# Storing the token difference feature-major and building the shifted inputs with one multiply-add

## The chip, the cores and the metric

The kernel runs on one core of a Trainium2 chip. The metric is device time in microseconds (us) of one execution. Three runs of the kernel before took 2236.38, 2239.85 and 2240.13 us; their median is 2239.85 us.

## The reference, cut to what matters

One inference step of two layers over 1024 prompt tokens and 8 sample tokens, 1024 features wide. Layer 0 ends in an output projection and a layer norm; its result `x` is the input of layer 1, a recurrent (RWKV-7) layer. That layer mixes every token with the token before it, six times with six weight vectors `mu`, and projects each mix:

```
x_prev = concatenate([shift_prev[:, None], x[:, :-1]], axis=1)      # the token before; a stored row for the samples
xsh = x[None] + (x_prev - x)[None] * mu[:, None, None, :]           # six shifted inputs
r, k, v, z = einsum('nbtd,nde->nbte', xsh[:4], w_rkvz)
w_raw = -softplus(-(w0 + tanh(xsh[4] @ w1) @ w2)) - 0.5             # "sigma" in the kernel
a = sigmoid(a0 + (xsh[5] @ a1) @ a2)
# then the recurrence over tokens, a group norm, a gate by z, the output projection and a layer norm
```

For the prompt the token before token 0 is zero; each of the 8 samples is one token whose predecessor is a row of `state_shift`.

## The kernel before, in words

The kernel has four phases, A to D. A and B compute layer 0 up to its branches, phase C its output projection and layer norm, phase D all of layer 1. The program is written in order and then reordered by a scheduler, engine by engine: each engine then works through its own fixed list, and waits at an instruction until its operands are there and the buffer that it writes is free. TensorE is PE, VectorE DVE, ScalarE ACT, GpSimd POOL; SP is the queue that issues most DMAs.

**Phase C** (`phase_c`) handles nine tiles, eight of 128 tokens and one of the 8 samples, in the order t = 0 to 8. For each it loads `x` and the branch outputs, splits them into a high and a low float32r part, does 48 matmuls of 512 columns (L1073 to L1075), the layer norm (`ln_core`, L1027 to L1036), the gain and bias on POOL (L1078, L1079), eight transposes on PE (L1090) that ACT copies out (L1091) as the feature-major tile `xt`, and one store of `xt` to the DRAM scratch `x1T` (L1094). `x1T` exists twice: half 0 for tokens 0 to 511, half 1 for the rest and the samples. The buffers of a tile (`x`, `h`, `xt` and others) come in pairs.

**Phase D** (`phase_d`) begins with five projections for half 0, in the order in which `FSEQ` interleaves them: k, sigma, r, a, v. After them the recurrence runs over 16 units, with the projections of half 1 and later the z projections and the output filled in between. Each projection starts with `xmake(h, i)` (from L1187): for each of the 8 blocks `k` of 128 features it loads 512 or 520 tokens of `x1T` into `xk` at column 1 (L1196), puts the predecessor of the first token into column 0 on POOL (L1198 zero, L1200 from `G.last`), scales on ACT by `1 - mu` into `xs` (L1201), adds `mu` times the neighbour column on DVE (L1202, and L1204 for the 8 samples), and splits the sum into `xh` (ACT, L1205) and `xl` (L1206, POOL, or DVE for every second block in the first five projections). `xmake` runs 12 times, 96 blocks in all. A projection k, r, v or z then takes 8 output blocks `j`, each with 8 x 3 matmuls per chunk of 256 tokens (L1178 to L1180), and stores each block (L1309).

A tile pool of phase D takes the bytes that earlier pools have left. A tile that lies on bytes of a phase C tile can be written only when that tile's last reader is done.

Of the kernel before, what the change touches and what calls it, by code (L numbers as in the profile page):

```python
# [8 lines left out]
F32 = mybir.dt.float32  # L9
# [1030 lines left out]
def phase_c(nc, tc, I, O, G):  # L1040
    ident = G.C["ident"]
    scr = G.scr
    with ExitStack() as es:
        pool = lambda name, bufs, **k: es.enter_context(tc.tile_pool(name=name, bufs=bufs, reuse_waits="tile", **k))
        one = pool("c1", 1)
        sp = pool("c2", 2)
        ps, woh, wol = G.ps, G.woh, G.wol
        gB = one.tile([128, D], F32, name="gB")
        bB = one.tile([128, D], F32, name="bB")
        nc.sync.dma_start(gB, I["ln_rows"][0:1].to_broadcast([128, D]))  # L1050
        nc.sync.dma_start(bB, I["ln_rows"][2:3].to_broadcast([128, D]))
        gT = one.tile([128, 2, 8], F32, name="gT")
        nc.sync.dma_start(gT, I["ln_cols"])
        for t in range(9):
            r = 128 if t < 8 else NS
            x = sp.tile([128, D], F32, name="x")
            nc.sync.dma_start(x[0:r], I["xp"][t * 128:t * 128 + 128] if t < 8 else I["xs"])
            yh = sp.tile([128, 8, 128], F32R, name="yh")
            yl = sp.tile([128, 8, 128], F32R, name="yl")
            y8 = sp.tile([128, 8, 128], F32, name="y8")  # L1060
            nc.sync.dma_start(y8[:, 0:4, 0:r], scr["ya"][:, :, t * 128:t * 128 + r])
            nc.sync.dma_start(y8[:, 4:8, 0:r], scr["yb"][:, :, t * 128:t * 128 + r])
            zt = sp.tile([128, 4, 128], F32, name="zt")
            nc.sync.dma_start(zt[:, :, 0:r], scr["za"][:, :, t * 128:t * 128 + r])
            nc.gpsimd.tensor_tensor(y8[:, 0:4, 0:r], y8[:, 0:4, 0:r], zt[:, :, 0:r], op=MUL)
            for i in (0, 4):
                sv = y8[:, i:i + 4, 0:r]
                split(nc, yh[:, i:i + 4, 0:r], yl[:, i:i + 4, 0:r], sv, nc.scalar, nc.vector if i else nc.gpsimd)
            a = ps.tile([128, 1024], F32, name="S")
            for n in range(2):  # L1070
                sl = slice(n * 512, n * 512 + 512)
                for k in range(8):
                    nc.tensor.matmul(a[0:r, sl], lhsT=yh[:, k, 0:r], rhs=woh[:, k, sl], start=k == 0, stop=False)  # L1073
                    nc.tensor.matmul(a[0:r, sl], lhsT=yh[:, k, 0:r], rhs=wol[:, k, sl], start=False, stop=False)
                    nc.tensor.matmul(a[0:r, sl], lhsT=yl[:, k, 0:r], rhs=woh[:, k, sl], start=False, stop=k == 7)  # L1075
            h = ln_core(nc, sp, a, x, r)
            x1 = x
            nc.gpsimd.tensor_tensor(x1[0:r], h[0:r], gB[0:r], op=MUL)  # L1078
            nc.gpsimd.tensor_tensor(x1[0:r], x1[0:r], bB[0:r], op=ADD)  # L1079
            nc.scalar.dma_start(scr["x1"][t][0:r], x1[0:r])  # L1080
            if t == 7:
                nc.scalar.dma_start(O["shift_p"], x1[127:128])
            if t == 8:
                nc.scalar.dma_start(O["shift_s"], x1[0:r])
            xt = sp.tile([128, 8, 128], F32, name="xt")
            for half in range(2):
                pt = ps.tile([128, 512], F32, name="mm")
                for kk in range(4):
                    k = half * 4 + kk
                    nc.tensor.transpose(pt[:, kk * 128:kk * 128 + r], h[0:r, k * 128:k * 128 + 128], ident[0:r, 0:r])  # L1090
                    nc.scalar.activation(xt[:, k, 0:r], pt[:, kk * 128:kk * 128 + r], AF.Identity,  # L1091
                                         scale=gT[:, 0, k:k + 1], bias=gT[:, 1, k:k + 1])
            q, c0 = (t // 4, (t % 4) * 128) if t < 8 else (1, 512)
            nc.sync.dma_start(scr["x1T"][q][:, :, c0:c0 + r], xt[:, :, 0:r])  # L1094
            if t == 3:
                nc.vector.tensor_copy(G.last, xt[:, :, 127:128])


def phase_d(nc, tc, I, O, G):
# [5 lines left out]
    with ExitStack() as es:  # L1105
# [20 lines left out]
        K = {k: cc[:, o:o + n] for k, (o, n) in G.offc.items()}  # L1126
        mu = one.tile([128, 6, 8], F32, name="mu")
        nc.sync.dma_start(mu, I["mu"])
        omu = one.tile([128, 6, 8], F32, name="omu")
        nc.vector.tensor_scalar(omu, mu, -1.0, 1.0, op0=MUL, op1=ADD)  # L1130
        shT = one.tile([128, 8, NS], F32, name="shT")
        nc.sync.dma_start(shT, I["shT"])
        vec = one.tile([128, 8, 7], F32, name="vec")
        nc.sync.dma_start(vec[:, :, 0:5], I["vec"])
        nc.vector.tensor_scalar(vec[:, :, 5:6], vec[:, :, 1:2], 0.5, None, op0=MUL)
# [51 lines left out]
        def xmake(h, i):  # L1187
# [3 lines left out]
            for k in range(8):  # L1191
                hi.append(xp.tile([128, 520], F32R, name="xh"))
                lo.append(xp.tile([128, 520], F32R, name="xl"))
                t = sp.tile([128, 520], F32, name="xs")
                x = one.tile([128, 528], F32, name="xk", bufs=3)
                nc.sync.dma_start(x[:, 1:1 + n], scr["x1T"][h][:, k, 0:n])  # L1196
                if h == 0:
                    nc.gpsimd.memset(x[:, 0:1], 0.0)  # L1198
                else:
                    nc.gpsimd.tensor_copy(x[:, 0:1], G.last[:, k])  # L1200
                nc.scalar.activation(t[:, 0:n], x[:, 1:1 + n], AF.Copy, scale=omu[:, i, k:k + 1])  # L1201
                nc.vector.scalar_tensor_tensor(t[:, 0:512], x[:, 0:512], mu[:, i, k:k + 1], t[:, 0:512], op0=MUL, op1=ADD)  # L1202
                if h:
                    nc.vector.scalar_tensor_tensor(t[:, 512:n], shT[:, k], mu[:, i, k:k + 1], t[:, 512:n], op0=MUL, op1=ADD)  # L1204
                nc.scalar.activation(hi[k][:, 0:n], t[:, 0:n], AF.Copy)  # L1205
                (nc.vector if early[0] and k % LD == 0 else nc.gpsimd).tensor_tensor(lo[k][:, 0:n], t[:, 0:n], hi[k][:, 0:n], op=SUB)  # L1206
            return hi, lo
# [332 lines left out]
        def sample_d():  # L1540
# [36 lines left out]
            sa = late.tile([128, 64], F32, name="sa")  # L1577
            y = late.tile([128, 64], F32, name="ys")
            for v0 in range(0, 64, 8):
                S = one.tile([128, 8, 64], F32, name="xk", bufs=3)  # L1580
                t = one.tile([128, 8, 64], F32, name="xk", bufs=3)
                vs = slice(v0, v0 + 8)
                kb = lambda i: R[:, i].unsqueeze(1).to_broadcast([128, 8, 64])
                vb = lambda a: a[:, vs].unsqueeze(2).to_broadcast([128, 8, 64])
# [117 lines left out]
        def t_out(g):  # L1702
# [19 lines left out]
                nc.sync.dma_start(h[ti], scr["x1"][2 * g + ti])  # L1722
            H = [[x[:, 0:512], x[:, 512:]] for x in h]
            if g == 2:
                H.append([one.tile([128, 512], F32, name="xk", bufs=3) for _ in range(2)])
                for f in range(2):
                    nc.sync.dma_start(H[2][f][0:NS], scr["x1"][8][0:NS, f * 512:f * 512 + 512])
            st = sp.tile([128, 3, 8], F32, name="st")
# [78 lines left out]
def body(tc, I, O, stage="all"):  # L1807
# [4 lines left out]
    with ExitStack() as es:  # L1812
# [7 lines left out]
        for nm, v in (("eps_ln", LN_EPS), ("eps_gn", GN_EPS), ("eps_kk", 1e-30)):  # L1820
            C[nm] = cp.tile([128, 1], F32, name=nm)
            nc.gpsimd.memset(C[nm], v)
        G.last = cp.tile([128, 8, 1], F32, name="last")
        G.scr = {"x1": [dp.tile([128, D], F32, name=f"x1_{t}") for t in range(9)],
                 "x1T": [dp.tile([128, 8, 512 + NS * q], F32, name=f"x1T_{q}") for q in range(2)],
                 **{k: dp.tile([128, 4, TT], F32, name=k) for k in ("ya", "za", "zb", "q", "yb")},
                 "sgs": dp.tile([NS, D], F32, name="sgs")}
        with ExitStack() as eC:
# [17 lines left out]
            phase_c(nc, tc, I, O, G)  # L1846
        if stage == "C":
            for q in range(2):
                nc.sync.dma_start(O["d_x1T"][:, :, q * 512:q * 512 + 512], G.scr["x1T"][q][:, :, 0:512])
            return  # L1850
        phase_d(nc, tc, I, O, G)

# [81 lines left out]
```

## Time and profile before

| what | us |
|---|---|
| median of three runs | 2239.85 |
| profiled execution: span from first to last instruction | 2226.9 |
| PE busy | 1841.2 (83%) |
| DVE busy | 1605.9 (72%) |
| ACT busy | 1145.9 (51%) |
| POOL busy | 1024.0 (46%) |
| DMA engines busy (main hardware queue) | 32.2% |

The page describes one execution; of its own time it gives the span, and the median of the runs is 12.95 us above that. Busy times are sums over stages with different limits, so the prediction reads stages, as windows of the span. Phase C begins on PE at about 880 us, the first matmul of phase D starts at 990.85 us, the recurrence at 1240 us, and the last `xmake` block is made at 1818 us.

### The profile page before, as it was taken

What the parts mean: (1) busy time and instruction counts of PE and PEld (TensorE: products, weight loads), DVE (VectorE), ACT (ScalarE), POOL (GpSimd) and SP (SyncE); (2) the same over time, 40 slices, a digit from 0 to 9 for tenths busy, and PEclk for the clock granted to TensorE, in tenths of its full rate; (3) what the DMA queues carried; (4) which work ended last, traced back from release to release, by engine and by line L of the source; (5) the groups of instructions that cost most, each with busy time, mean ns of one, the idle gap of its engine ahead of it and who ended that gap; (6) DMA issues with size and microseconds to landing.
All of it is one profiled execution on the core that took longest, in us unless ns stands there. A gap on an engine that the chain in (4) does not pass through costs nothing. (4 is left out here: it accounts for less than half of the span.)

```text
span 2226.9 us, 41589 instructions
## 1 busy us (share of the span) xinstructions
PE 1841.2 (83%) x15802; PEld 1536.7 (69%) x15802; DVE 1605.9 (72%) x3103; ACT 1145.9 (51%) x2279; POOL 1024.0 (46%) x877
## 2 busy tenths in 40 slices
PE   5988897668998996997779998789989967987944
PEld 4987896656767775766669886579878646765532
DVE  5998994558788886246364678976579899888453
ACT  3323324554665554467475557765564664554433
POOL 4667666545655544535345213344234354123333
PEclk8998998868999975998779997789899777997867
DMA  6424444521221115545566343454334434342532
GB/s 233 135 74 139 136 143 152 199 72 45 64 59 52 56 47 151 156 143 162 177 195 192 112 113 106 128 163 140 108 104 132 125 115 154 86 144 76 172 110 97
DMA packets 234657, 276.32 MB, mean 124 GB/s; under 512 B 72057, under 2 KB 174129, under 8 KB 230298
## 3 DMA queue, kind: packets, MB, share of 16 engines
q1 hardware_dynamic: 213272, 216.26, 32.2%
q0 software_dynamic: 7616, 41.52, 5.6%
q10 hardware_dynamic: 13570, 15.90, 2.0%
q8 instruction: 124, 2.03, 0.4%
q14 instruction: 75, 0.61, 0.1%
HBM read 213.52 MB, written 64.27 MB: 125 GB/s over the span
## 5 line engine op out<-in xcount | busy, mean ns | idle before, releaser
L121 POOL TENSOR_TENSOR wl<-w,wh 128x1024 fp32r<-128x1024 f32 x81 | 199.0, 2457 | 267.3 <-ACT wh L113 229.6
L1178 PE MATMUL mm<-xh,wh 128*128 128x256 f32 (+1 forms) x1024 | 306.7, 301 | 13.7 <-ACT og L1307 5.0
L1179 PE MATMUL mm<-xl,wh 128*128 128x256 f32 (+1 forms) x1024 | 305.0, 298 | 4.8 <-POOL xl L1206 4.1
L1180 PE MATMUL mm<-xh,wl 128*128 128x256 f32 (+1 forms) x1024 | 301.0, 294 | 0.0
L113 ACT ACTIVATE wh<-w 128x1024 fp32r<-128x1024 f32 (+2 forms) x130 | 134.5, 1034 | 188.8 <-DMA w<-in_w_fm 63.5
L1178 PEld LDWEIGHTS mm<-xh,wh 128*128 128x128 f32 x1024 | 200.7, 197 | 24.8 <-ACT og L1307 6.5
L1179 PEld LDWEIGHTS mm<-xl,wh 128*128 128x128 f32 x1024 | 202.1, 197 | 12.3 <-POOL xl L1206 4.9
L1180 PEld LDWEIGHTS mm<-xh,wl 128*128 128x128 f32 x1024 | 202.0, 197 | 4.8 <-issue 2.9
L268 DVE SCALAR_TENSOR_TENSOR c<-U,cw,c 128x1024 f32<-128x1024 f32 x120 | 198.1, 1674 | 0.9
L604 POOL TENSOR_TENSOR Pl<-PT,Ph 128x512 fp32r<-128x512 f32 (+1 forms) x102 | 131.5, 1293 | 142.0 <-DVE Ph L603 116.0
L252 POOL TENSOR_TENSOR cbuf<-cbuf 128x256 f32<-128x256 f32 (+2 forms) x72 | 131.6, 1835 | 86.9 <-ACT cbuf L250 83.9
L217 PE MATMUL S<-xh,wh 128*128 128x344 f32 (+1 forms) x432 | 147.0, 340 | 23.8 <-ACT wh L113 12.5
L219 PE MATMUL S<-xh,wl 128*128 128x344 f32 (+1 forms) x432 | 145.3, 336 | 17.2 <-POOL wl L121 11.5
L218 PE MATMUL S<-xl,wh 128*128 128x344 f32 (+1 forms) x432 | 146.1, 338 | 3.6 <-POOL xl L121 3.4
L250 ACT ACTIVATE cbuf<-cbuf,wrow 128x256 f32<-128x256 f32 x192 | 79.3, 496 | 111.4 <-DMA cbuf<-in_ccmp,cix 79.8
L1206 POOL TENSOR_TENSOR xl<-xs,xh 128x520 fp32r<-128x520 f32 (+1 forms) x76 | 104.0, 1371 | 54.6 <-ACT xh L1205 52.9
L1202 DVE SCALAR_TENSOR_TENSOR xs<-xk,mu,xs 128x512 f32<-128x512 f32 x96 | 95.7, 1000 | 45.0 <-ACT xs L1201 42.5
L1417 DVE TENSOR_TENSOR ut<-uc,MT 128x16 f32<-128x16 f32 (+14 forms) x240 | 109.9, 458 | 20.1 <-POOL MT L1411 11.0
L217 PEld LDWEIGHTS S<-xh,wh 128*128 128x128 f32 (+1 forms) x432 | 85.4, 198 | 25.8 <-ACT wh L113 24.6
L562 DVE TENSOR_REDUCE nm<-S 128x1 f32<-128x640 f32 (+7 forms) x128 | 88.3, 699 | 17.1 <-PE S L558 16.0
L219 PEld LDWEIGHTS S<-xh,wl 128*128 128x128 f32 (+1 forms) x432 | 84.9, 196 | 21.8 <-POOL wl L121 13.7
L121 DVE TENSOR_TENSOR wl<-w,wh 128x1024 fp32r<-128x1024 f32 x45 | 57.8, 1285 | 44.4 <-ACT wh L113 44.4
(605 smaller groups left out, 5539.1 us busy)
## 6 DMA issues: line engine op xcount, KB each, us to landing
w<-in_w_rkvz SPq DMA_DIRECT2D x64, 512.0 KB
w<-in_w_out SPq DMA_DIRECT2D x36, 512.0 KB
w<-in_w_fm SPq DMA_DIRECT2D x25, 512.0 KB
xk<-x1T SPq DMA_DIRECT2D x48, 260.0 KB
xk<-x1T SPq DMA_DIRECT2D x48, 256.0 KB
w<-in_w_out SPq DMA_DIRECT2D x16, 256.0 KB
x<-in_xp SPq DMA_DIRECT2D x8, 512.0 KB
x<-x ACTq DMA_DIRECT2D x8, 512.0 KB
```

The source lines that it names most:

```text
L113: nc.scalar.activation(hi, src, AF.Copy, **({} if scale is None else {"scale": scale}))
L121: e_lo.tensor_tensor(lo, src, hi, op=SUB)
L217: nc.tensor.matmul(dst, lhsT=wh[:, k, 0:n], rhs=xh[:, k, sl], start=k == 0, stop=False)
L218: nc.tensor.matmul(dst, lhsT=wh[:, k, 0:n], rhs=xl[:, k, sl], start=False, stop=False)
L219: nc.tensor.matmul(dst, lhsT=wl[:, k, 0:n], rhs=xh[:, k, sl], start=False, stop=k == 7)
L252: nc.gpsimd.tensor_tensor(bv[:, 0:n], bv[:, 0:n], bv[:, n:2 * n], op=ADD)
L268: e.scalar_tensor_tensor(c[:, i, 0:T], u[:, k:k + T], cwh[:, i, k:k + 1], c[:, i, 0:T], op0=MUL, op1=ADD)
L604: lambda: nc.gpsimd.tensor_tensor(Pl[:, 0:w], PT[:, 0:w], Ph[:, 0:w], op=SUB)]
L1178: nc.tensor.matmul(dst, lhsT=wh[:, k], rhs=xh[k][:, lo:hi], start=k == 0, stop=False)
L1179: nc.tensor.matmul(dst, lhsT=wh[:, k], rhs=xl[k][:, lo:hi], start=False, stop=False)
L1180: nc.tensor.matmul(dst, lhsT=wl[:, k], rhs=xh[k][:, lo:hi], start=False, stop=k == 7)
L1417: nc.vector.tensor_tensor(tmp[:, :, 0:i + 1], uc[:, :, 0:i + 1], Mv[:, 0:i + 1, i].unsqueeze(1).to_broadcast([128, 8, i + 1]), op=MUL)
```

## The change

Phase C computes, beside each `xt`, the difference `dt` = token before minus token, and stores it too: `x1T` gets a second plane. Seven eighths of the work is one POOL subtraction of neighbouring columns; the first column of a tile comes on DVE from `edge`, a copy of the last column of the tile before; the samples use `shT`, whose load moves from phase D to phase C. `xmake` then loads two planes and does one DVE multiply-add in place over all columns. The ACT scaling, the column 0 writes on POOL, the DVE piece for the samples, `omu`, `G.last` and the use of `xs` in `xmake` go. `xk` has 4 buffers instead of 3 and the new `xd` has 2. The scratch that the program keeps for descriptors of POOL's DMAs falls from its default of 16384 to 8192 bytes a partition.

```diff
 # phase_c
+        shT = one.tile([128, 8, NS], F32, name="shT")
+        nc.sync.dma_start(shT, I["shT"])
+        edge = one.tile([128, 8, 1], F32, name="edge", bufs=2)
+        nc.gpsimd.memset(edge, 0.0)
...
-            nc.sync.dma_start(scr["x1T"][q][:, :, c0:c0 + r], xt[:, :, 0:r])
-            if t == 3:
-                nc.vector.tensor_copy(G.last, xt[:, :, 127:128])
+            nc.sync.dma_start(scr["x1T"][q][:, 0, :, c0:c0 + r], xt[:, :, 0:r])
+            dt = sp.tile([128, 8, 128], F32, name="dt")
+            if t < 8:
+                nc.gpsimd.tensor_tensor(dt[:, :, 1:128], xt[:, :, 0:127], xt[:, :, 1:128], op=SUB)
+                nc.vector.tensor_tensor(dt[:, :, 0:1], edge, xt[:, :, 0:1], op=SUB)
+                edge = one.tile([128, 8, 1], F32, name="edge", bufs=2)
+                nc.vector.tensor_copy(edge, xt[:, :, 127:128])
+            else:
+                nc.vector.tensor_tensor(dt[:, :, 0:r], shT, xt[:, :, 0:r], op=SUB)
+            nc.sync.dma_start(scr["x1T"][q][:, 1, :, c0:c0 + r], dt[:, :, 0:r])
 # phase_d
-        omu = one.tile([128, 6, 8], F32, name="omu")
-        nc.vector.tensor_scalar(omu, mu, -1.0, 1.0, op0=MUL, op1=ADD)
-        shT = one.tile([128, 8, NS], F32, name="shT")
-        nc.sync.dma_start(shT, I["shT"])
 # phase_d, xmake, for each k
-                t = sp.tile([128, 520], F32, name="xs")
-                x = one.tile([128, 528], F32, name="xk", bufs=3)
-                nc.sync.dma_start(x[:, 1:1 + n], scr["x1T"][h][:, k, 0:n])
-                if h == 0:
-                    nc.gpsimd.memset(x[:, 0:1], 0.0)
-                else:
-                    nc.gpsimd.tensor_copy(x[:, 0:1], G.last[:, k])
-                nc.scalar.activation(t[:, 0:n], x[:, 1:1 + n], AF.Copy, scale=omu[:, i, k:k + 1])
-                nc.vector.scalar_tensor_tensor(t[:, 0:512], x[:, 0:512], mu[:, i, k:k + 1], t[:, 0:512], op0=MUL, op1=ADD)
-                if h:
-                    nc.vector.scalar_tensor_tensor(t[:, 512:n], shT[:, k], mu[:, i, k:k + 1], t[:, 512:n], op0=MUL, op1=ADD)
+                t = one.tile([128, 528], F32, name="xk", bufs=4)
+                e = one.tile([128, 520], F32, name="xd", bufs=2)
+                nc.sync.dma_start(t[:, 0:n], scr["x1T"][h][:, 0, k, 0:n])
+                nc.sync.dma_start(e[:, 0:n], scr["x1T"][h][:, 1, k, 0:n])
+                nc.vector.scalar_tensor_tensor(t[:, 0:n], e[:, 0:n], mu[:, i, k:k + 1], t[:, 0:n], op0=MUL, op1=ADD)
 # body, kernel
-                 "x1T": [dp.tile([128, 8, 512 + NS * q], F32, name=f"x1T_{q}") for q in range(2)],
+                 "x1T": [dp.tile([128, 2, 8, 512 + NS * q], F32, name=f"x1T_{q}") for q in range(2)],
-    nc = _bacc.Bacc("TRN2", target_bir_lowering=False, num_devices=1)
+    nc = _bacc.Bacc("TRN2", target_bir_lowering=False, num_devices=1, dynamic_dma_scratch_size=8192)
```

The scheduler also orders the border between the two phases anew. On PE, before, the projection matmuls of phase D (`mm<-xh,wh`, `mm<-xl,wh`, `mm<-xh,wl`) begin while matmuls (`S<-...`) and transposes (`mm<-ident,h`) of phase C are still to come; these rows stand where the first of them is:

```order
L1075 MATMUL S<-woh,yl 128x512
L1178 MATMUL mm<-xh,wh 128x256 x2
L1179 MATMUL mm<-xl,wh 128x256
L1180 MATMUL mm<-xh,wl 128x256
L1178 MATMUL mm<-xh,wh 128x256
L1179 MATMUL mm<-xl,wh 128x256
L1180 MATMUL mm<-xh,wl 128x256
L1178 MATMUL mm<-xh,wh 128x256
L1090 MATMUL mm<-ident,h 128x128
```

From the first projection matmul on, 48 matmuls and 33 transposes of phase C (one of them shown) still stand among those of phase D. On PE, in the changed program, the end of phase C and the first projection matmuls (L1185 to L1187 are the same three lines) read:

```order
L1094 MATMUL mm<-ident,h 128x128
L1079 MATMUL S<-woh,yl 8x512
L1094 MATMUL mm<-ident,h 128x128 x16
L1094 MATMUL mm<-ident,h 128x8 x8
L1185 MATMUL mm<-xh,wh 128x256 x2
L1186 MATMUL mm<-xl,wh 128x256
L1187 MATMUL mm<-xh,wl 128x256
```

All of phase C now stands ahead of all of phase D, on PE and on every other compute engine. On SP, before, the constants `cc` and `mu` are loaded ahead of phase C, and the first loads of `xk` stand between the loads and stores of phase C:

```order
L1094 DMA x1T_80<-xt 1024x1x128
L1196 DMA xk<-x1T_80 128x512 x6
L1057 DMA x<-in_xp 128x1024
L1196 DMA xk<-x1T_80 128x512
L1094 DMA x1T_81<-xt 1024x1x128
L1196 DMA xk<-x1T_80 128x512 x6
```

On SP, in the changed program, the same place (the two rows with `big` load rows of `x` for a later output projection):

```order
L1107 DMA x1T_80<-dt 128x8x8
L1107 DMA x1T_80<-dt 128x8x128
L1136 DMA cc<-in_cstc 128x640
L1139 DMA mu<-in_mu 128x48
L1141 DMA vec<-in_vec 128x8x5
L1203 DMA xk<-x1T_79 128x512
L1204 DMA xd<-x1T_79 128x512
L1203 DMA xk<-x1T_79 128x512
L1204 DMA xd<-x1T_79 128x512
L1203 DMA xk<-x1T_79 128x512 x2
L1723 DMA big<-x_0_70 128x1024
L1723 DMA big<-x_1_71 128x1024
```

The loads of `cc`, `mu` and `vec` and the first loads of `xk` and `xd` now stand behind the last store of `dt`. In the built program `cc`, `mu`, `vec` and two of the four `xk` buffers lie on bytes of the two `dt` buffers; before, no tile that `xmake` uses lay on a tile of phase C.

## Rows read from the trace of the kernel before

**Rows 1.** The page, part 1: span, busy time of engines.
```profile
span 2226.9 us, 41589 instructions
PE 1841.2 (83%) x15802; PEld 1536.7 (69%) x15802; DVE 1605.9 (72%) x3103; ACT 1145.9 (51%) x2279; POOL 1024.0 (46%) x877
```

**Rows 2.** The page, part 4: chain that ended last, by engine.
```profile
DVE 12%; PE 7%; DMA 3%; ACT 3%; issue 2%; SPq 1%; POOL 0%; POOLq 0%; DVEq 0%; ACTq 0%
```

**Rows 3.** Windows: PE, PEld, DVE, ACT, POOL busy, granted clock, DMA share, GB/s.
```profile
1043.00:1080.00 37.00, 21.55 (x78) 15.43 (x79) 18.53 (x25) 21.36 (x44) 10.74 (x13) 0.57 0.64 193
1135.00:1166.00 31.00, 16.69 (x71) 12.26 (x70) 18.61 (x25) 23.05 (x46) 11.58 (x15) 0.61 0.70 220
1191.00:1237.00 46.00, 44.76 (x379) 44.35 (x378) 20.12 (x21) 20.43 (x38) 24.74 (x22) 1.00 0.61 190
```

**Rows 4.** Windows of L1073 alone: PE and PEld busy (instructions), clock, DMA.
```profile
1010.00:1020.00 10.00, 0.00 (x0) 0.00 (x0) 0.83 0.53 167
```

**Rows 5.** Timeline of PE: start, duration, line, operation.
```profile
990.85 0.40 PE L1178 MATMUL mm<-xh,wh 128*128 128x256 f32 x2
...
1008.15 0.40 PE L1074 MATMUL S<-wol,yh 128*8 128x512 f32 x1
1008.39 0.39 PE L1075 MATMUL S<-woh,yl 128*8 128x512 f32 x1
```

**Rows 6.** Timeline of SP at the border of the two phases.
```profile
983.65 10.35 SPq L1196 DMA_DIRECT2D xk<-x1T  x6
...
1043.01 0.33 SPq L1309 DMA_DIRECT2D rk<-og  x1
...
1058.94 0.52 SPq L1094 DMA_DIRECT2D x1T<-xt  x1
```

**Rows 7.** Timeline of ACT there; in brackets idle time before, and releaser.
```profile
977.81 1.67 ACT L1091 ACTIVATE xt<-mm,gT 128x128 f32<-128x128 f32 x4
...
986.47 0.73 ACT L1201 ACTIVATE xs<-xk,omu 128x512 f32<-128x512 f32 x1 [1.72 <-DMA xk<-x1T]
987.43 0.73 ACT L1201 ACTIVATE xs<-xk,omu 128x512 f32<-128x512 f32 x1 [0.24 <-DMA xk<-x1T]
...
1040.60 0.61 ACT L1205 ACTIVATE xh<-xs 128x512 fp32r<-128x512 f32 x1
```

**Rows 8.** Timeline of DVE: first and last large operation of one layer norm.
```profile
977.72 0.69 DVE L1027 SCALAR_TENSOR_TENSOR h<-x,S 128x512 f32<-128x512 f32 x1 [7.69 <-PE mm L1090]
...
984.37 0.81 DVE L1036 TENSOR_SCALAR h<-h,st 128x1024 f32<-128x1024 f32 x1
```

**Rows 9.** Groups by line, 983 to 1240: count, busy, mean ns, idle before.
```profile
L1079 POOL TENSOR_TENSOR x<-x,bB 128x1024 f32<-128x1024 f32 (+1 forms) x4 | 10.3, 2574 | 0.1
```

**Rows 10.** Instructions of tiles xk and xs: duration ns min/median/max, first and last start.
```profile
L1201 ACT ACTIVATE xs<-xk,omu x96: 705/721/732, 986.5 to 1812.9; 128x512 f32<-128x512 f32 x48, 128x520 f32<-128x520 f32 x48
L1202 DVE SCALAR_TENSOR_TENSOR xs<-xk,mu,xs x96: 710/752/2898, 987.2 to 1818.0; 128x512 f32<-128x512 f32 x96
L1205 ACT ACTIVATE xh<-xs x96: 612/631/645, 988.3 to 1819.5; 128x512 fp32r<-128x512 f32 x48, 128x520 fp32r<-128x520 f32 x48
```

**Rows 11.** Timeline of SP: last two stores of projection v, half 0.
```profile
1231.50 0.32 SPq L1309 DMA_DIRECT2D rv<-og  x1
1237.09 0.32 SPq L1309 DMA_DIRECT2D rv<-og  x1
```

**Rows 12.** Groups by line, 1240 to 1830.
```profile
L1201 ACT ACTIVATE xs<-xk,omu 128x520 f32<-128x520 f32 (+1 forms) x45 | 32.2, 720 | 8.7 <-POOL xl L1206 7.0 <-DVE xh L1241 1.5
...
L1204 DVE SCALAR_TENSOR_TENSOR xs<-shT,mu,xs 128x8 f32<-128x8 f32 x37 | 14.7, 396 | 0.0
```

**Rows 13.** The page, part 5: line that waits for POOL's gathers.
```profile
L250 ACT ACTIVATE cbuf<-cbuf,wrow 128x256 f32<-128x256 f32 x192 | 79.3, 496 | 111.4 <-DMA cbuf<-in_ccmp,cix 79.8
```

More of the change, by code (lines that the diff above doesn't have):

```diff
@@ L1579, in sample_d @@
             for v0 in range(0, 64, 8):
-                S = one.tile([128, 8, 64], F32, name="xk", bufs=3)
-                t = one.tile([128, 8, 64], F32, name="xk", bufs=3)
+                S = one.tile([128, 8, 64], F32, name="xk", bufs=4)
+                t = one.tile([128, 8, 64], F32, name="xk", bufs=4)
                 vs = slice(v0, v0 + 8)
@@ L1724, in t_out @@
             if g == 2:
-                H.append([one.tile([128, 512], F32, name="xk", bufs=3) for _ in range(2)])
+                H.append([one.tile([128, 512], F32, name="xk", bufs=4) for _ in range(2)])
                 for f in range(2):
@@ L1822, in body @@
             nc.gpsimd.memset(C[nm], v)
-        G.last = cp.tile([128, 8, 1], F32, name="last")
         G.scr = {"x1": [dp.tile([128, D], F32, name=f"x1_{t}") for t in range(9)],
-                 "x1T": [dp.tile([128, 8, 512 + NS * q], F32, name=f"x1T_{q}") for q in range(2)],
+                 "x1T": [dp.tile([128, 2, 8, 512 + NS * q], F32, name=f"x1T_{q}") for q in range(2)],
                  **{k: dp.tile([128, 4, TT], F32, name=k) for k in ("ya", "za", "zb", "q", "yb")},
@@ L1848, in body @@
             for q in range(2):
-                nc.sync.dma_start(O["d_x1T"][:, :, q * 512:q * 512 + 512], G.scr["x1T"][q][:, :, 0:512])
+                nc.sync.dma_start(O["d_x1T"][:, :, q * 512:q * 512 + 512], G.scr["x1T"][q][:, 0, :, 0:512])
             return
```

## The prediction

> **What bounds the kernel now.** I read the busy shares first: PE 83% and DVE 72% of the span, no engine full [rows 1]. So the kernel is bound by different things in different stages, and an average of busy time says little. The chain that ended last covers only about 28% of the span before it breaks off; inside it DVE has 12 parts of 28, PE 7, ACT and DMA 3 each [rows 2]. That is the recurrence, from about 1590 us to the end. For the earlier stages I read windows. The reader is to see two kinds [rows 3]: from 1191 to 1237, while projection v runs, PE is busy 44.8 of 46 us at full clock, its higher level (2.4 GHz); from 1043 to 1080 and from 1135 to 1166, the sigma and a stages, PE is busy 21.6 of 37 and 16.7 of 31 us, and the granted clock falls to 0.57 and 0.61, most of the way to the lower level. There PE waits for what others prepare.
>
> Last I read the border of phases C and D, which the change touches most. The first projection matmul starts at 990.85, the last matmul of C's output projection at 1008.39 [rows 5]; behind 1010 there is none [rows 4]. The last store of C goes out at 1058.94 [rows 6]. So for 68 us the two phases share the engines: C's matmuls keep PE busy while `xmake` builds the first inputs, and C's last norms and evictions fill gaps of D.
>
> **The change, part by part.**
>
> *The border.* In the changed order all of C stands ahead of all of D, and `mu`, `vec`, two `xk` buffers and `cc` must wait for the `dt` buffers. I follow the last tiles. When PE reaches 990.85, C has 48 matmuls and 33 transposes to go. The matmuls follow each other in 0.24 us (1008.15 to 1008.39 [rows 5]): 11.5 us; nine of the transposes lie between them, some 2 us by my estimate. Matmuls end at 1004.3. Sixteen transposes for tiles 6 and 7 come next, and eight short ones for tile 8. They are paced by ACT's evictions, 1.67/4 = 0.42 us each [rows 7]: tile 6 ends 3.3 us later, 1007.6, and frees the `h` buffer that tile 8's norm needs. That norm takes from 977.72 to 985.18, 7.5 us, when nothing delays it [rows 8]: 1015.1. On POOL the gain of tile 8 now stands before the last `dt`; each is about a 1024-element operation of 2.57 us [rows 9]: 1020.3. The store is issued in 0.52 us and lands after about 2.8 us, which I take from the first `xk` load, issued at 983.65 and there at 986.47 [rows 6, 7]: 1023.6. Then SP issues `cc`, `mu`, `vec`, `xk`, `xd` at 0.33 us each; `xd` starts at 1025.0 and is there at 1027.8. With 0.75 us for the multiply-add and 0.63 for `xh` [rows 10] the first projection matmul starts near 1029, 38 us later than before.
>
> *The pace behind it.* Not all of the 38 us is lost, because before the first 16 blocks (k and sigma) were slow: from 983.65 to 1041.2, where the sixteenth `xh` ends [rows 6, 7], 3.6 us a block. After the change nothing of C competes, and a block costs ACT 0.63 and DVE 0.75 plus half an `xl`. The limit becomes the loads. The second load of a row of six lands 0.96 us behind the first [rows 7], so two planes take 1.9 us a block; and `xd` has two buffers, so a buffer's round of issue, landing and use, 0.33 + 2.8 + 0.75, gives 3.9/2 = 1.9 as well. Fifteen blocks further on, with 3.8 us for the two 512 KB `big` loads that stand between them and 1.4 for the last multiply-add and `xh`, it is 1027.8 + 28.5 + 3.8 + 1.4 = 1061.5, 20 us later than 1041.2. The other mark agrees: projection k's blocks are ready at 1046.3, three more output blocks at 5.6 us each (1231.50 to 1237.09 [rows 11]) put the fourth `rk` store at 1064 instead of 1043.01 [rows 6]. I take **+20**. Bounds: if the last store lands without the wait on POOL and blocks go at the engines' own 1.1 us, about +1; if each block waits its whole round of 3.9 us, +50. The value lies nearest to the row that shows loads in flight together.
>
> The Trainium skill (SBUF — State Buffer, section The DMA setup-cost knee) says that every transfer pays about 2 us that do not grow with its bytes, and takes 436 GB/s for the rest; 256 KB would be an estimated 2.6 us. For the first landing, 2.8 us, the trace agrees; for the next one, 0.96 us behind, it does not, since the fixed part overlaps. By the page with no overlap the sixteen blocks' loads alone would come to an estimated 83 us.
>
> *The sigma stage.* C's last evictions and its last norm lie inside 1043 to 1080 before, up to the store at 1058.94 [rows 3, 6]. One tile's eight evictions are 3.3 us of ACT. Without them I credit **-5**, between 0 and -8.
>
> *The r and a stages.* Their blocks gain ACT's 0.72 us [rows 10] but load twice as much into two buffers. Eight blocks that fetch at 1.9 instead of 0.96 us lose up to 7.5; most of a's lie beside r's matmuls. I take **+3**, between 0 and +8. Everything up to the recurrence is one sequence, so these terms shift all that follows.
>
> *The rest of D.* From 1240 to 1830, 45 blocks shed 32.2 us of ACT scaling and 14.7 us of DVE's sample piece [rows 12]. What of it counts I take from the chain's shares [rows 2]: 12/28 of 14.7 is 6.3, 3/28 of 32.2 is 3.4, together -9.7. The 45 further loads, 0.96 us each, are 43 us of transfer, of which 3/28, +4.6, should show. **-5**, between -47 (all of it on the path) and +43 (each load waited for). POOL's column 0 writes are off the chain, as POOL has 0% there; their cover is POOL's own idle time.
>
> *Phases A, B and C proper.* Their orders are unchanged up to C. `dt` adds eight POOL operations of 2.57 us and nine stores to C; PE's queue of matmuls hides them, except the last, counted above. The halved descriptor scratch could delay POOL's gathers, for which ACT already waits 79.8 us [rows 13]: I take 0, with +8 (a tenth of that wait) as upper end; nothing makes it a gain.
>
> Sum: 20 - 5 + 3 - 5 = **+13 us** on a span of 2226.9. The median of the runs lies 12.95 us above that span, and I leave this as it is: **2253 us**, 0.6% slower. From no change a measurement of this kernel can tell about 0.2%, 4.5 us.
>
> **The rivals.**
>
> *The border is nearly free (faster).* The stage is bound by DVE and ACT, not by loads: before, a block took 3.6 us because norms and POOL's long operations stood in its way, and DVE's L1202 reached 2.9 us [rows 10]. If blocks run at 1.1 us, the border costs +1; with -5 in sigma, 0 in r and a, and -10 in the rest the sum is -14: 2226 us. It decides from the point where the sixteenth `xh` of the new kernel ends before about 1048. Against it stand the in-order loads behind the last `dt` store. Chance 0.2.
>
> *It cancels.* Blocks go at 1.4 us, between the two paces, so the border costs +12; sigma -5, r and a +3, and the rest of D keeps its -9.7 because the further loads are fetched early enough: 2240 us. For it speaks that DMA ended so little of the chain [rows 2]. Chance 0.15.
>
> *The loads stall DVE in the recurrence.* DVE's queue is in order; before, ACT stood between the load and DVE, now the multiply-add itself waits for `xd`, and behind it stand the steps of the recurrence. If each of the 45 loads is waited for at 0.96 us, +43 replaces +4.6: 2253 + 38 = 2291 us. Against it: SP fetches ahead by two blocks. Chance 0.08.
>
> The Trainium skill (Perfetto Trace Analysis, section Optimization Strategy) advises interleaving stages that are limited by different engines. It gives no price; the rows above show what the interleaving hid, and the forecast charges for it.
>
> **How the numbers follow.** The forecast, 2253, has 0.57 and its own range 2242 to 2268. The range for 8 in 10 reaches down over the cancelling case to 2229 and up to 2280; most of the first and third rivals, about 2 in 10, stays outside. Slower by over 0.2%: the forecast but for its lower edge, the third rival and some of the cancelling case, 0.63. Within 0.2%: 0.16. Faster: 0.21.
>
> **What would show it.** In the changed kernel's trace the first projection matmul stands near 1029 behind all of C, PE idles some 20 us before it at a falling clock, the sixteenth `xh` ends near 1061, the fourth `rk` store goes out near 1064, and the first unit of the recurrence starts near 1258 instead of 1240. If that start has moved by less than 8 us the border is mispriced; if it has moved by 18 and the total has not grown, the rest of D is. A PE that runs projection matmuls among C's transposes would make the order, and with it the main term, wrong. If DVE shows waits for `xd` behind 1260, the third rival holds.

## The result, and the profile after

The changed kernel took 2310.36 us (median of 4 runs, 2306.93 to 2311.48), the kernel before beside it 2239.85 (median of three; a fourth run, at 2338.53 us, was in a slow state and is left out). The measured ratio is 1.0365, with a 95% interval of 1.032 to 1.041, which is 82 us. These two medians are only 70 us apart, a ratio of 1.0315, but in a later round the kernel before ran between 2218.41 and 2244.22 us (23 runs, median 2228.1), 82 under the changed one. I go by the measured ratio. The direction was forecast, the size (+13, with a range up to +40) was not. The profiled execution is 78.3 us longer than before's.

The page, parts 1 and 4, answers to [rows 1, 2]:

```profile
span 2305.2 us, 41422 instructions
PE 1870.6 (81%) x15802; PEld 1561.2 (68%) x15802; DVE 1619.6 (70%) x3070; ACT 1088.5 (47%) x2183; POOL 1031.0 (45%) x790
...
DVE 6%; PE 5%; DMA 2%; ACT 2%; issue 1%; SPq 1%; POOL 0%; POOLq 0%; DVEq 0%; ACTq 0%
```

ACT lost 57 us of work, and the span grew. Three marks cut the span: the first matmul of C's output projection (885.4 before, 894.7 after), the first matmul of the recurrence (L1377; L1378 after; 1240.3 and 1286.2), and the end. From C to the recurrence it was 354.9 us and is 391.5, +36.6; from there to the end 986.7 and 1018.9, +32.2; 9.3 us lie ahead of C.

The border, on PE (timeline: start, duration, line, operation; in brackets the idle time before and what ended it), answers to [rows 5]:

```profile
1038.39 0.27 PE L1094 MATMUL mm<-ident,h 8*128 8x8 f32 x1 [0.45 <-ACT xt L1095]
1052.95 0.79 PE L1185 MATMUL mm<-xh,wh 128*128 128x256 f32 x2 [14.29 <-ACT xh L1206]
```

Between the last transpose of C and the first projection of D nothing runs on PE. The end of C on DVE, with the first and the last large operation of tile 8's norm and the last of tile 7's:

```profile
1024.34 0.67 DVE L1027 SCALAR_TENSOR_TENSOR h<-x,S 8x512 f32<-8x512 f32 x1
...
1026.79 0.79 DVE L1036 TENSOR_SCALAR h<-h,st 128x1024 f32<-128x1024 f32 x1
...
1032.94 0.80 DVE L1036 TENSOR_SCALAR h<-h,st 8x1024 f32<-8x1024 f32 x1
1034.92 3.16 DVE L1102 TENSOR_TENSOR dt<-edge,xt 128x8 f32<-128x8 f32 x1 [1.18 <-ACT xt L1095]
```

On POOL, the last subtraction and the first instruction of D:

```profile
1036.17 1.87 POOL L1101 TENSOR_TENSOR dt<-xt 128x1016 f32<-128x1016 f32 x1
...
1045.65 0.10 POOL L1146 MEMSET zo<- 128x1 f32 x1 [5.30 <-DMA x1T<-dt]
```

And on SP, the last stores of C and the first loads of D:

```profile
1040.47 0.98 SPq L1107 DMA_DIRECT2D x1T<-dt  x2
1045.58 0.35 SPq L1136 DMA_DIRECT2D cc<-in_cstc  x1
...
1047.12 0.65 SPq L1203 DMA_DIRECT2D xk<-x1T  x1
1047.81 0.68 SPq L1204 DMA_DIRECT2D xd<-x1T  x1
```

The norm of tile 8 ends 6.15 us behind that of tile 7 (L1036 twice). The stores of `dt` are issued at 1040.47; POOL and SP, whose next instructions write bytes that `dt` held, wait until 1045.6 for them to land. Then `xk` is loaded, and the first `xh` ends at 1052.90.

Windows of the sigma stage, the a stage and projection v, answering to [rows 3]; columns as there:

```profile
1090.00:1127.00 37.00, 23.59 (x128) 19.20 (x128) 15.23 (x23) 14.94 (x28) 5.86 (x4) 0.68 0.65 222
1179.00:1212.00 33.00, 14.43 (x46) 10.56 (x47) 19.66 (x25) 18.00 (x38) 12.33 (x7) 0.53 0.82 274
1238.00:1284.00 46.00, 45.21 (x382) 45.01 (x381) 14.96 (x15) 16.82 (x32) 20.56 (x13) 1.00 0.70 228
```

In the a stage DMA is busy 0.82 of the time where it was 0.70, and the granted clock is 0.53; projection v runs on PE as before.

The multiply-add among the groups by line (count, busy, mean ns, idle before and its releasers), from 1040 to 1286:

```profile
L1205 DVE SCALAR_TENSOR_TENSOR xk<-xd,mu,xk 128x512 f32<-128x512 f32 (+1 forms) x53 | 47.7, 917 | 51.4 <-DMA xd<-x1T 46.4 <-DMA xk<-x1T 4.1 <-issue 0.5
```

And from 1286 to 2092:

```profile
L1205 DVE SCALAR_TENSOR_TENSOR xk<-xd,mu,xk 128x520 f32<-128x520 f32 (+1 forms) x43 | 32.7, 770 | 1.6 <-DMA xk<-x1T 1.1 <-POOL xl L1207 0.5
```

Up to the recurrence DVE waits 46.4 us for `xd`; behind it, for 43 blocks, hardly at all. So the third rival, loads that stall DVE in the recurrence, is out for this kernel, and yet the recurrence is 32 us longer. Its window in the changed kernel, columns as above:

```profile
1286.20:2305.00 1018.80, 825.98 (x9346) 661.46 (x9345) 759.27 (x1729) 512.07 (x994) 347.05 (x316) 0.83 0.43 128
```

And in the kernel before, with the same 9346 matmuls:

```profile
1240.30:2226.90 986.60, 812.13 (x9346) 650.17 (x9345) 746.20 (x1768) 540.84 (x1039) 348.48 (x358) 0.84 0.40 121
```

### The profile page after: what moved, and what is told of

Its sections match the earlier page's. It is cut to its first block, busy times and chain, and to the rows that moved or that the text cites. A ratio compares the mean times of both kernels' runs of the same rounds, so it can differ in the third digit from the quotient of the medians.

```text
span 2305.2 us, 41422 instructions
## 1 busy us (share of the span) xinstructions
PE 1870.6 (81%) x15802; PEld 1561.2 (68%) x15802; DVE 1619.6 (70%) x3070; ACT 1088.5 (47%) x2183; POOL 1031.0 (45%) x790
## 5 line engine op out<-in xcount | busy, mean ns | idle before, releaser
L1185 PE MATMUL mm<-xh,wh 128*128 128x256 f32 (+1 forms) x1024 | 310.1, 305 | 34.2 <-ACT xh L1206 23.7
L1187 PE MATMUL mm<-xh,wl 128*128 128x256 f32 (+1 forms) x1024 | 305.6, 299 | 0.0
L1185 PEld LDWEIGHTS mm<-xh,wh 128*128 128x128 f32 x1024 | 203.5, 200 | 47.2 <-ACT xh L1206 25.2
L1187 PEld LDWEIGHTS mm<-xh,wl 128*128 128x128 f32 x1024 | 204.6, 200 | 5.5 <-issue 2.7
L1207 POOL TENSOR_TENSOR xl<-xk,xh 128x520 fp32r<-128x520 f32 (+1 forms) x76 | 107.9, 1435 | 93.7 <-ACT xh L1206 85.1
L1205 DVE SCALAR_TENSOR_TENSOR xk<-xd,mu,xk 128x512 f32<-128x512 f32 (+1 forms) x96 | 80.4, 851 | 53.0 <-DMA xd<-x1T 46.4
L1206 ACT ACTIVATE xh<-xk 128x512 fp32r<-128x512 f32 (+1 forms) x96 | 58.4, 629 | 92.2 <-DVE xk L1205 88.8
```

The source lines that it names most:

```text
L1185: nc.tensor.matmul(dst, lhsT=wh[:, k], rhs=xh[k][:, lo:hi], start=k == 0, stop=False)
L1187: nc.tensor.matmul(dst, lhsT=wl[:, k], rhs=xh[k][:, lo:hi], start=False, stop=k == 7)
```

## The experiments

The question was where 82 us come from: the separation of C and D at the border, the doubled loads, the work and stores of `dt`, the halved scratch, or something in the recurrence that the prediction had not looked at. The table gives every run: the ratio to the kernel before with its 95% interval, and from each run's one profiled execution, by its timelines, the start of C's matmuls, the way from there to the first D matmul, to the sixteenth `xh` and to the first matmul of the recurrence, and from that to the end (us). Both `xh` and matmul are taken at their start. A profile is one execution, which took up to 8 us more or less than the median of its kernel's runs, e4's 15 more; a difference of a few us between two rows can be that.

| kernel | ratio | C starts | to first D | to 16th `xh` | to recurrence | recurrence to end |
|---|---|---|---|---|---|---|
| before | 1 | 885.4 | 105.4 | 155.2 | 354.9 | 986.7 |
| after | 1.0365 [1.032, 1.041] | 894.7 | 158.2 | 193.2 | 391.5 | 1018.9 |
| e1 half scratch | 1.0016 [0.9992, 1.004] | 891.6 | 105.7 | 156.4 | 355.9 | 986.1 |
| e2 C part, overlapping | 1.0277 [1.0234, 1.032] | 892.2 | 158.8 | 193.7 | 387.2 | 1002.5 |
| e3 C part, apart | 1.0223 [1.0182, 1.0263] | 891.7 | 105.2 | 157.6 | 363.9 | 1030.7 |
| e4 change, apart | 1.0217 [1.0177, 1.0258] | 903.1 | 108.6 | 161.8 | 370.0 | 1019.8 |
| e5 old work, e3's order | 1.0178 [1.0128, 1.0227] | 889.6 | 106.4 | 156.3 | 359.8 | 1026.7 |
| e6 C part, old order | 1.0056 [1.0022, 1.0091] | 897.2 | 105.0 | 157.3 | 363.3 | 989.8 |
| e7 change, old order | 1.0072 [1.0046, 1.0099] | 891.5 | 108.8 | 164.2 | 367.0 | 985.6 |
| e8 e2, old order | 1.0198 [1.0148, 1.0248] | 899.2 | 171.4 | 203.9 | 400.3 | 978.6 |
| e9 nine small copies | 1.006 [1.0034, 1.0086] | 890.2 | 104.0 | 153.4 | 353.6 | 993.0 |
| e10 e7, few loads | 0.9991 [0.9964, 1.0019] | 898.6 | 108.7 | 160.5 | 352.9 | 966.5 |
| e11 whole change, old order | 1.0244 [1.0203, 1.0284] | 895.1 | 165.4 | 201.7 | 406.4 | 986.6 |
| e12 old work, third order | 1.0133 [1.0095, 1.017] | 887.3 | 104.1 | 159.2 | 355.6 | 1008.6 |

**First round: which part of the change.** e1 is the kernel before with the scratch alone:

```diff
-    nc = _bacc.Bacc("TRN2", target_bir_lowering=False, num_devices=1)
+    nc = _bacc.Bacc("TRN2", target_bir_lowering=False, num_devices=1, dynamic_dma_scratch_size=8192)
```

> The kernel before with the DMA descriptor scratch halved to 8192 bytes and nothing else; every engine has the same instructions in the same order. Theory (the lost time is in the border of C and D and in the loads): 2240 us, within 0.3% of before, and the first C matmul at 885 us. Rival (the 9 us that the changed kernel is late at the start of phase C come from the smaller scratch, through the gathers): 2247 to 2252 us, the first C matmul at 890 or later, and the gathers' landings longer than before's.

Measured: 2235.78 us, a ratio that does not differ from 1, as the theory had it; but C starts at 891.6 in the profile, as the rival had it. The rival's mechanism is not seen: POOL's gathers into `cbuf` land after 7.0 us in the median, before's after 7.1. The mark moves from run to run: 885.4 to 890.2 in the four profiles with the whole scratch, 891.5 to 903.1 in the ten with half of it. So the scratch may cost some us ahead of C; the interval of the ratio allows up to 9, and this stays open. It is not where the 82 us are.

e2 has the C half of the change alone, e3 the same with `dt` away from D's tiles:

```diff
+            dt = sp.tile([128, 8, 128], F32, name="dt")
...
+            nc.sync.dma_start(scr["x1T"][q][:, 1, :, c0:c0 + r], dt[:, :, 0:r])
...
-                nc.sync.dma_start(x[:, 1:1 + n], scr["x1T"][h][:, k, 0:n])
+                nc.sync.dma_start(x[:, 1:1 + n], scr["x1T"][h][:, 0, k, 0:n])
 # e3 only
-PAD = 128
+PAD = 1690
```

> The half of the change that is in phase C alone: the difference is computed and stored, D computes its inputs as before and never reads it. As in the changed kernel the dt buffers lie on the addresses of D's constants and xk, so that no C matmul stands behind the first D matmul on TensorE. Theory A (the border costs because the order of C and D is separated): first D matmul at 1035 to 1055, 2270 to 2290 us. Rival B (the doubled loads cost, the separation is made up for): 2240 to 2250 us.

Measured: 2290.46 us, half a microsecond above theory A's range; first D matmul at 1051.07. The border behaves as in the changed kernel, with before's single loads: from the first D matmul to the sixteenth `xh` it takes 34.9 us, the changed kernel with its doubled loads 35.0.

> The same as the run before it, but a larger pad moves D's constants and xk behind the end of the dt buffers: C and D interleave as in the kernel before (48 C matmuls behind the first D matmul). Theory A (separation): the difference's own work and its 4.2 MB of stores cost under 8 us, 2240 to 2250 us, some 30 us under the overlapping form. Rival B (loads): the same as the overlapping form within 6 us. Rival C (the stores and the subtractions in C themselves hold up D): 2265 or more and no gain against the overlapping form.

Measured: 2281.02 us. Theory A had said at most 2250. At the border e3 is as before (first D matmul 105.2 us behind C's start), and still it loses 50 us, 44 of them in the recurrence, whose code and data are those of before. Rival B's 6 us are missed by little, but D loads nothing twice here; rival C's total fits, but it puts the loss into the start of D, where it is not. All three theories fell on this run.

e4 is the whole change with one `dt` buffer and a pad that keeps it off D's tiles:

```diff
-PAD = 128
+PAD = 650
...
-            dt = sp.tile([128, 8, 128], F32, name="dt")
+            dt = sp.tile([128, 8, 128], F32, name="dt", bufs=1)
```

> The whole change, with one dt buffer in place of two and a larger pad, so that dt does not lie on D's constants and xk: C and D interleave again. Theory A (separation costs 37 us of the 70, the loads the rest): 2265 to 2280 us, first D matmul before 1010. Rival B (loads cost all of it): 2300 to 2312 us. Rival D (the separation costs everything, the loads nothing): 2235 to 2245 us.

Measured: 2279.25 us, just inside theory A's range, though the first D matmul came at 1011.75 and not before 1010, C having begun late. It is no slower than e3, which loads one plane only. What e3 and e4 share is a new order: given other work in C, the scheduler orders the recurrence anew. To get from before's list to e3's, at least 1939 of PE's 7455 and 624 of DVE's 1884 instructions of phase D have to be moved.

**Second round: the order held fixed.** A table of each engine's order in phase D is put into the program, as an edge from every instruction to the one that is to stand behind it; no edge is a wait.

```diff
+        n0 = len(nc.cur_bb.bb.instructions)
         phase_d(nc, tc, I, O, G)
+        as_written(nc, tc, n0)
...
+            if last is not None:
+                tc.add_manual_dep(ins[at], ins[last].name, info, reason="order")
```

e5 puts e3's order on the kernel before; e6, e7 and e8 put before's order on e3, e4 and e2 (in e7 the loads of `xk` and `xd` are left to the scheduler).

> The kernel before, with the same instructions, buffers and scratch; only the order in which each engine works through phase D is that of e3_c_part_apart, held by a table. Theory (order: the scheduler, given some more work in phase C, orders the recurrence anew, and that order is the worse one): 2265 to 2285 us, the start of the recurrence within 5 us of before and the loss behind it. Rival (work: the stores and subtractions in C, or the moved addresses, cost 45 us): 2228 to 2240 us.

Measured: 2275.22 us, in the theory's range and 1.8% slower, with before's operations and pools. What the order brings with it is small: ACT loads its function tables twice more (2281 ACT instructions against 2279, 1.28 us each), and in the built program 56 tiles of phase D take another buffer of their own set. The loss is in the recurrence, 1026.7 against 986.7 us; its start lies 4.9 us later behind C's. Its window; that of before stands above:

```profile
1249.40:2276.00 1026.60, 832.84 (x9346) 662.81 (x9345) 750.73 (x1768) 542.78 (x1041) 349.81 (x358) 0.82 0.38 116
```

The waits of DVE in that window of e5 (us in total, times, longest):

```profile
DVE kk L1337 <- ACT inv L1336: 25.7, 11, 6.4
...
DVE SV L1506 <- PE pB L1478: 17.5, 5, 6.0
...
DVE big L1745 <- PE mm L1741: 15.1, 3, 10.2
```

And in that of before:

```profile
DVE kk L1337 <- ACT inv L1336: 9.8, 7, 2.9
...
DVE SV L1506 <- PE pB L1478: 4.9, 3, 2.2
...
DVE big L1745 <- PE mm L1741: 1.7, 1, 1.7
```

DVE is busy 746 and 751 us, so it stands still 240 us before and 276 in e5. In the new order it comes to `kk`, to the state update and to the output's residual before their operands are there, and what stands behind them waits too; this is read from one profile each. PE's clock falls from 0.84 to 0.82, and the same 9346 matmuls take 21 us more.

> e3_c_part_apart (the difference computed and stored in C, not read by D, no overlap) with every engine's order in phase D as in the kernel before. Theory (order): 2233 to 2248 us, as before but for up to 10 us of C. Rival (work): 2275 to 2285 us, no change against e3.

Measured: 2248.74 us, 0.7 us above the range of the order theory; without its new order e3 is 1.7% faster.

> e4_change_apart (the whole change, dt away from D's constants) with every engine's order in phase D as before, the removed instructions taken out of it and only the loads of xk and xd left to the scheduler. It prices the doubled loads less the shed work. If these are worth nothing at one order: 2235 to 2250 us. If the loads cost (the first 16 blocks at 1.9 us or more, DVE waiting for xd): 2255 to 2275 us. If order has no part in it: 2279 as e4.

Measured: 2248.54 us, in the range for doubled loads and shed work that cancel. The whole change costs 0.72% at the old order and with C and D interleaved. Its recurrence takes 985.6 us, as before's:

```profile
1258.50:2244.00 985.50, 811.12 (x9346) 647.94 (x9345) 733.19 (x1731) 513.84 (x994) 337.84 (x316) 0.84 0.44 133
```

> e2_c_part_overlapping (dt on the addresses of D's constants, D reads as before) with every engine's order in phase D as before. It prices the separation of C and D alone. If the separation costs what the start of D shows (first D matmul 50 us later, about 32 us of it left at the start of the recurrence in e2): 2262 to 2275 us. If that is made up for later: 2235 to 2248 us. If order has no part in it: 2290 as e2.

Measured: 2279.00 us, a little above the range, 1.0198 against e6's 1.0056: the separation alone costs 1.4%, about 32 us. In the profiles it is 37.0 us at the recurrence (400.3 against 363.3), and 11 of them come back behind it (978.6 against 989.8). On PE the gap at the border is 26 us wide here:

```profile
1043.91 0.27 PE L1094 MATMUL mm<-ident,h 8*128 8x8 f32 x1 [0.45 <-ACT xt L1095]
1070.58 0.80 PE L1191 MATMUL mm<-xh,wh 128*128 128x256 f32 x2 [26.40 <-ACT xh L1218]
```

**Third round: how much is luck, what the loads cost, do the terms add up.** e9 adds to C nine copies that nothing reads:

```diff
+        tiny = one.tile([128, 8, 1], F32, name="tiny")
...
+            nc.vector.tensor_copy(tiny[0:r], xt[0:r, :, 0:1])
```

> The kernel before with one DVE copy of 8 elements a partition behind each of the nine stores of phase C, some 0.6 us of DVE in all; nothing reads them. The scheduler orders phase D anew: 671 of PE's 7455 and 236 of DVE's 1884 instructions of D change their place. If the order before is one good draw among many: slower by 10 to 40 us, 2245 to 2275 us. If only some orders are bad: within 8 us of before, 2228 to 2242 us.

Measured: 2243.55 us, ratio 1.006, between the two ranges. The copies as instructions of the tile that they write (duration ns min/median/max, first and last start):

```profile
L1096 DVE COPY tiny<-xt x9: 156/160/1912, 933.7 to 1061.9; 128x8 f32<-128x8 f32 x8, 8x8 f32<-8x8 f32 x1
```

Together they are 4.3 us of DVE, more than I had said, since two of them took 1.2 and 1.9; but C and the way to the recurrence are no longer for them (353.6 us against 354.9). The recurrence is, by 6 us (993.0 against 986.7), no more than profiles at one order differ by (978.6 to 989.8 at before's, with D's work as before).

> The kernel before with phase D in a third order, the one that the scheduler draws for e3's program when the subtraction runs on DVE in place of POOL; work, buffers and scratch are as before. If orders drawn anew are as a rule worse: 2250 to 2285 us. If e3's order was an unlucky one: 2228 to 2245 us.

Measured: 2261.57 us, in the range for new orders being worse, 1.3% slower, again with before's operations alone. Of four orders of one work (e9's copies apart), before's is the fastest, and the other three cost 0.6 to 1.8%.

e10 leaves out 84 of the 96 loads of the difference:

```diff
-                e = one.tile([128, 520], F32, name="xd", bufs=2)
+                e = one.tile([128, 520], F32, name="xd", bufs=2) if k < 1 else e
...
+                if k < 1:
                     nc.sync.dma_start(e[:, 0:n], scr["x1T"][h][:, 1, k, 0:n])
```

> e7_change_old_order without 84 of the 96 loads of the difference: each xmake loads one block and uses it eight times, so the result differs and everything else stays. If the second loads cost the 11 to 13 us that e7 loses at the start of D: 2232 to 2240 us, the sixteenth xh 10 us or more earlier behind the start of C than in e7, and the recurrence no faster. If the stores and subtractions of C cost them: 2245 to 2252 us, as e7.

Measured: 2225.60 us, below either range: the time of before, and by the ratios 0.8%, some 18 us, under e7. So the second loads cost what e7 loses. But I had put that cost into the first blocks: the sixteenth `xh` comes only 4 us earlier behind C's start than in e7, and the recurrence, which I had expected no faster, takes 966.5 us against 985.6. The multiply-add among the groups by line up to the recurrence, in e7:

```profile
L1205 DVE SCALAR_TENSOR_TENSOR xk<-xd,mu,xk 128x512 f32<-128x512 f32 (+1 forms) x51 | 51.5, 1021 | 36.6 <-DMA xd<-x1T 33.0 <-DMA xk<-x1T 2.2 <-POOL xl L1207 1.2
```

In e10, where the line is L1206, and below it the window of e10's recurrence:

```profile
L1206 DVE SCALAR_TENSOR_TENSOR xk<-xd,mu,xk 128x512 f32<-128x512 f32 (+1 forms) x51 | 54.2, 1086 | 14.3 <-DMA xk<-x1T 7.4 <-DMA xd<-x1T 6.8
```

```profile
1251.50:2218.00 966.50, 799.38 (x9346) 639.56 (x9345) 731.23 (x1731) 512.13 (x994) 338.20 (x316) 0.85 0.41 125
```

The idle time before the multiply-add falls from 36.6 to 14.3 us, and 14 us of that show at the recurrence (367.0 against 352.9). In the recurrence itself, first e7, then e10:

```profile
L1205 DVE SCALAR_TENSOR_TENSOR xk<-xd,mu,xk 128x520 f32<-128x520 f32 (+1 forms) x45 | 41.4, 922 | 11.2 <-DMA xd<-x1T 9.1 <-issue 1.8
```

```profile
L1206 DVE SCALAR_TENSOR_TENSOR xk<-xd,mu,xk 128x520 f32<-128x520 f32 (+1 forms) x45 | 40.7, 911 | 0.2
```

At before's order DVE waits 9.1 us for `xd` in e7's recurrence, in five waits, and not at all in e10's. So about half of the 19 us is what the third rival described; the rest is not settled, as one profile each, at 0.84 and 0.85 of the clock, tells too little.

> The changed kernel as it is, dt lying on D's constants, with every engine's order in phase D as before (the loads of xk and xd left to the scheduler). If the terms add up (change at the old order +14, separation +30): 2274 to 2288 us, so that 25 to 35 us of the changed kernel's loss are the new order of the recurrence. If the separation alone brought the loss: 2300 to 2312 us.

Measured: 2285.81 us, where the added terms had put it. The changed kernel with before's order in D is 1.2% faster than as the scheduler made it, and its recurrence takes 986.6 us instead of 1018.9. But up to the recurrence it takes 406.4 us, 15 more than the changed kernel.

**The account**, in ratios to before: the change itself at the old order, C and D interleaved, +0.7% (16 us; e7), the separation of C and D at that order +1.7% (38 us; e11 less e7, which has one `dt` buffer; without the loads 1.4%, e8 less e6), the new order of D +1.2% (27 us; after less e11, two rounds apart; in the form without overlap, e4 less e7, it is 1.45%; with the 1.0315 of after's own round it would be 0.7%). The three steps follow on each other, so they give 3.65% by construction; what supports them is that the second and the third, taken in another form, agree to 0.3%. The third is a balance: the new order takes 15 us less up to the recurrence than before's order does where C and D are separated (391.5 against 406.4; without the loads 387.2 in e2 against 400.3 in e8), and 32 us more behind it. So how much is the separation's and how much the order's depends on the order at which the separation is priced. e10 divides the first step: without the second loads +0, so the loads +0.8%; and since the work in C alone costs 0.6% (e6), the shed operations of ACT, POOL and DVE give about that back. No version that does all the work of the change beat the kernel before; the nearest is e7.

## Why the prediction was wrong, step by step

The span grew by 78.3 us where +13 was forecast. Of the 65 us between, 37 lie in the rest of D, 18 at the border and 9 ahead of C.

**The rest of D, forecast -5, measured +32: the step that failed.** The prediction priced 45 shed operations and 45 loads by their shares of the chain in before's trace, and its bounds, -47 to +43, were made of these alone. Both bounds took it that the recurrence runs in the order of before; that +32 lies between them is luck, since the upper one stood for loads that are waited for. At before's order the term is right to within 5 us: -1.1 in e7, -0.1 in e11. That is luck in part too: without the loads the recurrence takes 966.5 us (e10), so the loads were nearer +19 than +4.6 and the shed operations nearer -20 than -9.7, as far as one profile each can tell. But the changed kernel has another order there, in which the recurrence takes 32 us more than at before's (1018.9 against 986.6 in e11), and e5 and e12 show that an order alone moves it by 22 to 40 us. The prediction looked at the order of the border, where a reason to look was plain, and not at that of the 1000 us behind it. Its sum priced operations; a list that an engine works through in order can wait at other places though no operation changed.

**The border, forecast +20, measured +38 at the sixteenth `xh`** (193.2 against 155.2 us behind C's start), +36.6 at the recurrence, where the sum of border, sigma, r and a had said +18. The mechanism was right: all of C ahead of all of D, a gap on PE, only a part of it won back. The sizes were not. The first D matmul came 52.8 us later behind C's start, not 38. Some 11 of these 15 us arise before the last store is issued. Moved by the 9.3 us that C began later, the prediction has tile 8's norm run from 1016.9 to 1024.4 and the store issued at 1029.6; in the trace it ran from 1024.34 to 1033.74, and the store was issued at 1040.47. On ACT and DVE the norms of tiles 7 and 8 and the evictions of tile 6 had gone on among each other, each of which the prediction took at its undisturbed length. Then the last stores took 5.1 us to land where I took 2.8 from a load, and the first pair of loads needed 4.4 us from the issue of `xk` to the multiply-add (1047.12 to 1051.48). And the blocks came at 2.4 us (1052.3 to 1088.0 for fifteen), not 1.9. DVE waited for `xd` 46.4 us up to the recurrence, but that the loads set this pace, as the prediction had it, is not shown: e2, with single loads and ACT's scaling kept, came at the same pace. The fourth `rk` store went out at 1094.74, not near 1064. The Trainium skill (Perfetto Trace Analysis, section Optimization Strategy) advises interleaving regimes; the trace agrees, and e8 gives the price here.

**The sigma, r and a stages, forecast -2 together, measured -1.4** (38.0 at the sixteenth `xh`, 36.6 at the recurrence): right, and in its parts too, -6 up to the twenty-fourth `xh` (forecast -5) and +5 from there (forecast +3).

**A, B and C proper, forecast 0 with +8 as upper end.** The profile shows 9.3 us more ahead of C, e1's ratio +0.16% with an interval that holds both 0 and 9 us: not settled. A part is clock: from 489 to 511 PE had 0.77 before and 0.50, its lower level (1.2 GHz), after, with the same instructions in the same order, and got through 33 matmuls less. The scratch alone does not decide this: in the ten profiles with half of it the clock there lies anywhere from 0.50 (e4, e8) to 0.84 (e11). The window of before, then that of after:

```profile
489.00:511.00 22.00, 21.22 (x140) 19.50 (x140) 13.40 (x51) 7.97 (x23) 2.94 (x3) 0.77 0.00 1
```

```profile
489.00:511.00 22.00, 22.00 (x107) 22.00 (x106) 6.89 (x25) 5.58 (x15) 1.50 (x2) 0.50 0.00 1
```

**The rivals.** Nearly free (2226) and cancelling (2240) are out: the sixteenth `xh` ended at 1088.6, not before 1048. The loads that stall DVE in the recurrence gave the time nearest to the result (2291) for a reason that the changed kernel's trace denies, 1.1 us of such waits; at before's order there are 9.1 us of them (e7), a fifth of what the rival charged. Loads do cost, but e7 and e10 put all of them at 0.8%. The Trainium skill (SBUF — State Buffer, section The DMA setup-cost knee) charges about 2 us a transfer that do not grow with its bytes; with no overlap, 84 loads would by its figures be an estimated 218 us. The 18 us that e10 wins show that most of it is overlapped.

## What to carry to other kernels

In a program that a scheduler orders, compare the order of all stages behind the change, not of the changed ones alone; a difference of 1% between two versions may be the order's and none of the edit's. To price an edit, hold the order fixed; to price an order, put it on the old work. Before adding a tile near the end of a phase, look which bytes the next phase's first tiles take: lying on each other, the phases can't interleave.

## What was not expected

Nine copies of 8 elements a partition, read by nobody, cost 0.6%. One of them took 1.9 us where the median was 0.16, and a subtraction of 8 elements a partition took 3.16 us on DVE (L1102 at 1034.92) and ended with POOL's subtraction beside it, at 1038.0; another of the same form, at 1025.68, took 0.99. Whether POOL held it up was not tried, but the trace points to it: of the eight such subtractions of the changed kernel, two took 0.17 us, and the six others, 0.70 to 3.16 us long, all ended 0.03 to 0.04 us behind a subtraction of POOL. One of the pairs:

```profile
1017.28 1.17 DVE L1102 TENSOR_TENSOR dt<-edge,xt 128x8 f32<-128x8 f32 x1
```

```profile
1016.53 1.88 POOL L1101 TENSOR_TENSOR dt<-xt 128x1016 f32<-128x1016 f32 x1 [1.33 <-ACT xt L1095]
```

And the start of phase C, with the same instructions of PE ahead of it in one order, lay anywhere between 885 and 903 us.
